# Left sides stored one pair later, residual rows fetched one by one, low parts on VectorE: a decoder block on one core

## The chip, the cores and the metric

One core of a Trainium2 chip runs the kernel. The metric is device time in microseconds (us) of one execution; lower is better. Engines are named as in the profile: PE is TensorE (matmuls), DVE VectorE, ACT ScalarE, POOL GpSimd, SP the engine whose queue issues nearly all DMAs.

## The reference, cut to what matters

A decoder block: an SSD branch and a differential-attention branch are gated and merged, `w_out` adds them to the residual stream `h`, and a SwiGLU FFN and a last norm follow. The change touches the FFN alone, in float32, with 1024 tokens, `D_MODEL` = 1024 and `D_FF` = 2816:

```python
    h = h + merged @ w_out[l]
    u2 = rmsnorm(h, norm_ffn_g[l])
    h = h + (jax.nn.silu(u2 @ w_gate_ffn[l]) * (u2 @ w_up_ffn[l])) @ w_down_ffn[l]
out = rmsnorm(h, norm_final_g)
return out[:, PAD_FRONT + N_META:]
```

## The kernel before, in words

**Precision.** A float32 product is made of three fp32r matmuls: an operand is cast to a high part (hi, whi, dhi) on ACT, and the difference, the low part (lo, wlo, dlo), is made on POOL or DVE; hi by hi, lo by hi and hi by lo go into the same PSUM bank. `split_to(dst, src, eng)` (L919 the cast, L920 the low part on engine `eng`) does this.

**Gate and up.** The 2816 hidden columns are 11 pairs of 128 columns. For each pair `Weights` loads the 1024 x 256 block of `w_gate_ffn` or `w_up_ffn` in two halves (L948), `raw` tiles of 512 KB. The halves make a 2 x 2 block matrix (A11, A12, A21, A22), the tokens, normed and transposed, another, and the block product is made with seven products in place of eight, as Strassen's method does. `Weights.make` builds the seven left operands: 1, 2, 5, 6 and 7 are sums or differences of two blocks (L986, on DVE, into a `sm` tile), 3 and 4 are blocks themselves; each goes through `split_to`, with POOL for the low part. `Half.product` (L1000) runs the 12 matmuls (128 x 512) of one product, and `Half.run` adds the products' banks into the quarter tiles (L1015 on ACT, L1017 to L1026 on DVE). Product 3 goes into the bank of product 5, so it waits until L1017 has read that bank; likewise product 7 waits for L1022, and product 4 for L1015. `gate_out` takes silu on ACT (L1039 to L1042), `up_out` multiplies (L1045 to L1048). A pair is 168 matmuls.

**Left sides of down.** The down product too is made with seven products, from blocks of the hidden matrix G (pairs by token halves). `left_sides` makes five sums of its quarters on DVE (L1058, L1061, L1063 to L1065) and stores seven row blocks in the DRAM tile `hid_d`: three of 256 KB (L1059, L1062, L1066) and one of 1 MB (L1067).

**Down.** 77 steps: products 1, 5, 4, 7, 3, 2, 6, each over the 11 pairs. A step loads a row block of `hid_d` (`ra`, L1250) and one or two quarters of `w_down_ffn` (`rb`, L1259 and L1262), sums the quarters (L1270), splits both and runs 12 matmuls. Steps 0 to 2 are loaded and made in the last pair, and steps 3 and 4 are loaded there; the others use the pool `dn`, opened after step 2's matmuls. Its tiles are the eight residual rows `hr` (512 KB each, from `h_d`, L1347), the final gain `gf` (L1350), five `ra` and `rb` buffers, four of `dhi` and `dlo`. When a product's 11 steps are done, its banks are added into the rows (L1363), one addition a step of the next product. In the loop `dn_load(s + 4)` loads four steps ahead.

**What sets the order.** Tiles are allocated from rings of a few buffers: `raw` of the first weight half has two, of the second one (ring `ht`, four of whose five hold a token side), G and U two, `tmp` three, and a write waits for the last reader of the old content. A scheduler orders the instructions of each engine at build time. On the chip each engine runs its list in that order, and so does SP with the DMAs.

Of the kernel before, what the change touches and what calls it, by code (L numbers as in the profile page):

```python
# [9 lines left out]
F32 = mybir.dt.float32  # L10
F32R = mybir.dt.float32r
AF = mybir.ActivationFunctionType
ALU = mybir.AluOpType
# [4 lines left out]
P = 128  # L18
D = 1024
# [4 lines left out]
NT = SEQ // P  # L24
# [18 lines left out]
def tile_hybrid_block(  # L43
# [7 lines left out]
    nc = tc.nc  # L51
# [9 lines left out]
    def nm(s):  # L61
        seq[0] += 1
        return f"{s}_{seq[0]}"
# [69 lines left out]
    h_d = dram([SEQ, D], "h_d")  # L133
    hid_d = dram([7, FF // 2, 512], "hid_d")
# [113 lines left out]
    def gates_block(b):  # L248
# [9 lines left out]
        out=gbh, in0=par[:, PR_GB : PR_GB + 16], scalar1=0.5, scalar2=None, op0=ALU.mult  # L258
# [3 lines left out]
        out=g08, in0=par[:, PR_SUB : PR_SUB + 1], scalar1=1.0 - LAM_INIT, scalar2=None,  # L262
# [4 lines left out]
    with tc.tile_pool(name="ssd", bufs=1, reuse_waits="tile") as sp:  # L267
# [4 lines left out]
        def t2(name, tag="t2", bufs=4):  # L272
# [6 lines left out]
            out=tri, in_=tri, pattern=[[1, P]], compare_op=ALU.is_ge, fill=0.0, base=0,  # L279
# [637 lines left out]
    def split_to(dst, src, eng):  # L917
        hi, lo = dst
        nc.scalar.copy(hi, src)  # L919
        eng.tensor_tensor(out=lo, in0=src, in1=hi.bitcast(F32), op=ALU.subtract)  # L920
# [15 lines left out]
    class Weights:  # L936


        def __init__(self, w, pair):
            self.w, self.pair, self.m, self.two_ = w, pair, {}, {}  # L940
            self.load()
# [30 lines left out]
        def make(self, *which):  # L972
            for i in which:
                self.m[i] = dst = self.slot(i)
                if i in (3, 4):
                    split_to(dst, (self.A11, self.A22)[i - 3], nc.gpsimd)
                    continue
                a, b, op = {
                    2: (self.A21, self.A22, ALU.add),
                    5: (self.A11, self.A12, ALU.add),  # L980
                    1: (self.A11, self.A22, ALU.add),
                    6: (self.A21, self.A11, ALU.subtract),
                    7: (self.A22, self.A12, ALU.subtract),
                }[i]
                tmp = tmp512("sm").rearrange("p (k c) -> p k c", c=P)
                vtt(out=tmp, in0=a, in1=b, op=op)  # L986
                split_to(dst, tmp, nc.gpsimd)

    class Half:

# [41 lines left out]
    def gate_banks():  # L1032
        return ps_mm(), ps_mm(), ps_sc(), ps_sc()
# [18 lines left out]

    SLOT = {1: 0, 2: 1, 5: 2, 6: 3, 3: 4, 4: 5, 7: 6}

    def left_sides(G, U, pair):
        rows = slice(pair * P, (pair + 1) * P)
        a11, a12, a21, a22 = G[:, 0, T1], G[:, 1, T1], G[:, 0, T2], G[:, 1, T2]
        vtt(out=U[:, 0, T2], in0=a21, in1=a22, op=ALU.add)  # L1058
        nc.sync.dma_start(hid_d[SLOT[4], rows, :], a22)  # L1059
        d = fp.tile([P, 512], F32, tag="tmp", name=nm("d"), bufs=3)  # L1060
        vtt(out=d, in0=a12, in1=a22, op=ALU.subtract)  # L1061
        nc.sync.dma_start(hid_d[SLOT[7], rows, :], d)  # L1062
        vtt(out=U[:, 0, T1], in0=a11, in1=a22, op=ALU.add)  # L1063
        vtt(out=U[:, 1, T1], in0=a11, in1=a12, op=ALU.add)
        vtt(out=U[:, 1, T2], in0=a21, in1=a11, op=ALU.subtract)  # L1065
        nc.sync.dma_start(hid_d[SLOT[3], rows, :], a11)  # L1066
        nc.sync.dma_start(  # L1067
            hid_d[0:4, rows, :].rearrange("s p t -> p s t"),
            U.rearrange("p a (b t) -> p (a b) t", t=512),
        )  # L1070

    def w_out_rows(t, before_last=None):
        hts = []
# [81 lines left out]
    G, U = new_pair()  # L1155
# [83 lines left out]
    up_w.make(7)  # L1239
    up.run(7)  # L1240
    up_out(G, U, up, 0)
    left_sides(G, U, 0)

    NP = NF // 2
    downs = [(i, f) for i in (1, 5, 4, 7, 3, 2, 6) for f in range(NP)]
# [51 lines left out]
    for pair in range(1, NP):  # L1297
        G, U = new_pair()
        last = pair == NP - 1
        for w in (w_gate_ffn, w_up_ffn):  # L1300
            gate_side = w is w_gate_ffn
            A = Weights(w[0], pair)
            A.make(*order7)
            h = Half(A, G if gate_side else U, (gate_banks if gate_side else up_banks)())
            if last and not gate_side:
                for s, pool in ((0, st), (1, wk)):
                    down_load(s, f512(fp, "tmp", 3), f1k(st, "raw", 2))
                    down_make(s, f512(fp, "tmp", 3), *pair_of(pool))
                h.run(*order7[:5])
                down_load(2, f512(fp, "tmp", 3), f1k(st, "raw", 2))  # L1310
                down_make(2, f512(fp, "tmp", 3), *pair_of(st))
                h.run(*order7[5:])
                for s in (3, 4):
                    down_load(s, f512(st, "gt", 2), f1k(st, "raw", 2))
            else:
                h.run(*order7)
            if gate_side:
                gate_out(G, h)
            else:
                up_out(G, U, h, pair)  # L1320
                left_sides(G, U, pair)

    b4 = gate_banks()
    for s in range(3):
        down_mm(downs, b4, [(s, j) for j in range(4)])
# [4 lines left out]
    with tc.tile_pool(name="dn", bufs=1, side="right", reuse_waits="tile") as dn:  # L1330
# [7 lines left out]
        def dn_load(s):  # L1338
            if s < len(downs) and s > 4:
                down_load(s, f512(dn, "ra", 5), f1k(dn, "rb", 5))  # L1340
# [2 lines left out]
        dn_make(4)  # L1343
        rows = []
        for r in range(NT):
            ht = dn.tile([P, D], F32, name=f"hr{r}")
            nc.sync.dma_start(ht, h_d[r * P : (r + 1) * P, :])  # L1347
            rows.append(ht)
        gf = dn.tile([P, D], F32, name="gf")
        nc.sync.dma_start(gf, norm_final_g.partition_broadcast(P))  # L1350
        for s in range(5, 9):
            dn_load(s)
        parts = {
            1: ((0, 0, 1), (1, 1, 1)), 2: ((1, 0, 1), (1, 1, -1)), 3: ((0, 1, 1), (1, 1, 1)),
            4: ((0, 0, 1), (1, 0, 1)), 5: ((0, 0, -1), (0, 1, 1)), 6: ((1, 1, 1),),
# [28 lines left out]
        def store(r, n):  # L1384
            nc.sync.dma_start(out2[r * P : (r + 1) * P, N2[n]], jks[r][:, N2[n]])
# [17 lines left out]
        for p in range(7):  # L1403
            i = downs[p * NP][0]
            banks = b4 if p == 0 else (up_banks if p % 2 else gate_banks)()
            for f in range(3 if p == 0 else 0, NP):
                s = p * NP + f
                dn_load(s + 4)
                if s + 2 < len(downs) and s + 2 > 4:
                    dn_make(s + 2)  # L1410
                if p < 6 or f < NP - 2:
                    down_mm(downs, banks, [(s, j) for j in range(4)])
                elif f == NP - 1:
                    down_mm(downs, banks, [(q, j) for j in range(4) for q in (s - 1, s)])
                for _ in range(2 if i in (2, 6) else 1):
                    if later:
                        later.pop(0)()
            for t, n, sign in parts[i]:
                for j in range(4):
                    if p < 6:  # L1420
                        later.append(
                            lambda a=(i, banks[j], j, t, n, sign): add_part(*a)
                        )
            if i == 3:
                later += [lambda r=r: first_rows(r) for r in range(4)]
            if i == 2:
                for j in range(4):
                    later.append(lambda r=4 + j: (square(r, 0), gain(r, 0, nc.gpsimd)))
# [62 lines left out]
```

## Time and profile before

| what | value |
|---|---|
| median of 3 runs | 2026.34 us (2026.12 to 2028.18) |
| the profiled execution, its own time | 2029.1 us |
| its span, first to last instruction | 2026.7 us |
| PE, DVE, ACT, POOL busy | 1923.2, 1252.8, 762.1, 567.1 us |
| mean granted clock of PE | 0.983 |
| DMA bytes | 241.38 MB |

The span runs from the first instruction to the last; the execution's own time has 2.4 us around it. A view by windows gives each engine's busy time in stretches of the span, with the clock that PE was granted (1.00 is 2.4 GHz, 0.50 is 1.2). A view by time lists an engine's instructions with the idle time before each, and what released it. A matmul's end is modelled: the distance from start to start is its pace.

### The profile page before, as it was taken

The numbers are of one execution on the slowest core, as the hardware profiler recorded it, in microseconds if no ns is written. First come the engines' busy times: TensorE is split into PE (matmuls) and PEld (weight loads), VectorE is DVE, ScalarE is ACT, GpSimd is POOL, SyncE is SP. The second block draws the span as 40 slices with busy tenths as digits, with TensorE's granted clock in tenths as the row PEclk, the third lists the DMA queues.
The fourth block names the chain that finished last, engine by engine and source line by source line (L and its number), as shares of the span: only waits on it lengthen the run. The fifth ranks groups of instructions, "written<-read, shape, count | busy, mean of one in ns | idle before, by whom it ended". The sixth has DMA issues, their size and how long they took to land.

```text
span 2026.7 us, 27727 instructions
## 1 busy us (share of the span) xinstructions
PE 1923.2 (95%) x10478; PEld 1668.0 (82%) x10478; DVE 1252.8 (62%) x2387; ACT 762.1 (38%) x1443; POOL 567.1 (28%) x363
## 2 busy tenths in 40 slices
PE   7999999999999999999999999889999998969998
PEld 7999777789999999888978899767777776758886
DVE  5656678555766566654663443585566656648887
ACT  5333222245555455553331124532222222224454
POOL 2223444411111111110122244344444544400002
PEclk9999999999999999999999999999999999989999
DMA  5111344311111211123765444322322232368865
GB/s 174 49 33 53 97 140 133 112 45 50 53 45 46 61 51 40 51 68 121 253 226 173 151 156 160 111 89 84 93 78 92 80 113 85 114 250 304 313 218 198
DMA packets 185935, 241.38 MB, mean 119 GB/s; under 512 B 13517, under 2 KB 128442, under 8 KB 185802
## 3 DMA queue, kind: packets, MB, share of 16 engines
q1 hardware_dynamic: 185658, 239.09, 36.7%
q8 instruction: 82, 1.34, 0.3%
q10 hardware_dynamic: 144, 0.52, 0.1%
q14 instruction: 51, 0.42, 0.1%
HBM read 181.48 MB, written 53.84 MB: 116 GB/s over the span
## 4 chain that ended last, share of the span: by engine, by line
PE 77%; DVE 13%; DMA 6%; issue 1%; ACT 1%; POOL 0%; SPq 0%; DVEq 0%; POOLq 0%; ACTq 0%
PE mm L108 14%; PE mm L109 14%; PE mm L110 14%; PE sc L1000 5%; PE tp L1000 4%; DVE sm L986 3%; DMA raw<-in_w_up_ffn_dram 3%; PE mm L1000 3%; PE sc L109 2%; PE sc L108 2%; PE sc L110 2%; PE tp L729 2%; PE sc L681 1%; PE sc L684 1%; PE sc L529 1%
## 5 line engine op out<-in xcount | busy, mean ns | idle before, releaser
L89 POOL TENSOR_TENSOR wlo<-raw,whi 128x1024 fp32r<-128x1024 f32 x68 | 176.4, 2594 | 685.8 <-ACT whi L87 614.3
L108 PE MATMUL mm<-uTh,whi 128*128 128x346 f32 (+2 forms) x1008 | 360.4, 358 | 7.5 <-DVE kl L626 2.4
L109 PE MATMUL mm<-uTh,wlo 128*128 128x346 f32 (+2 forms) x1008 | 359.5, 357 | 0.0
L110 PE MATMUL mm<-uTl,whi 128*128 128x346 f32 (+2 forms) x1008 | 358.8, 356 | 0.0
L108 PEld LDWEIGHTS mm<-uTh,whi 128*128 128x128 f32 x1008 | 190.9, 189 | 28.5 <-issue 8.4
L110 PEld LDWEIGHTS mm<-uTl,whi 128*128 128x128 f32 x1008 | 191.0, 189 | 18.7 <-issue 3.9
L109 PEld LDWEIGHTS mm<-uTh,wlo 128*128 128x128 f32 x1008 | 190.9, 189 | 17.7 <-issue 3.4
L920 POOL TENSOR_TENSOR wlo<-sm,whi 128x512 fp32r<-128x512 f32 x88 | 129.7, 1493 | 161.9 <-ACT whi L919 161.9
L919 ACT CAST whi<-sm 128x512 fp32r<-128x512 f32 x88 | 52.7, 619 | 215.4 <-DVE sm L986 95.8
L700 ACT ACTIVATE S<-S,mx 128x272 f32<-128x272 f32 (+7 forms) x128 | 101.0, 791 | 54.7 <-DVE mx L696 53.1
L986 DVE TENSOR_TENSOR sm<-raw,raw 128x512 f32<-128x512 f32 x66 | 54.6, 864 | 67.8 <-DMA raw<-in_w_up_ffn_dram 64.5
L920 POOL TENSOR_TENSOR lo<-raw,hi 128x512 fp32r<-128x512 f32 x44 | 65.5, 1488 | 88.8 <-ACT hi L919 88.8
L87 ACT CAST whi<-raw 128x1024 fp32r<-128x1024 f32 x68 | 71.2, 1047 | 50.6 <-PE mm L110 41.9
L748 DVE TENSOR_TENSOR atl<-tp,ath 128x512 fp32r<-128x512 f32 (+1 forms) x80 | 50.5, 634 | 61.8 <-ACT ath L747 61.5
L986 DVE TENSOR_TENSOR sm<-raw 128x512 f32<-128x512 f32 x44 | 50.6, 1154 | 58.7 <-DMA raw<-in_w_gate_ffn_dram 37.7
L1000 PE MATMUL mm<-t2a,hi 128*128 128x512 f32 x176 | 65.8, 433 | 21.8 <-DVE gu L1017 17.7
L919 ACT CAST dhi<-ra 128x512 fp32r<-128x512 f32 x72 | 44.7, 621 | 109.8 <-issue 53.6
L689 DVE CUSTOM_DVE_ANT_0 S<-sc,base 128x272 f32<-128x272 f32 (+7 forms) x128 | 62.0, 493 | 28.2 <-PE sc L684 27.0
L681 PE MATMUL sc<-k,q 128*128 128x144 f32 (+6 forms) x224 | 76.7, 349 | 1.7 <-ACT S L700 1.1
L689 DVE CUSTOM_DVE_ANT_0 S<-sc,base,mx 128x348 f32<-128x348 f32 (+4 forms) x96 | 56.1, 585 | 34.6 <-PE sc L684 31.2
L108 PE MATMUL mm<-whi,uTh 128*128 128x256 f32 x256 | 73.9, 290 | 3.5 <-ACT whi L100 3.3
L109 PE MATMUL mm<-whi,uTl 128*128 128x256 f32 x256 | 74.8, 293 | 0.1
(398 smaller groups left out, 5200.7 us busy)
## 6 DMA issues: line engine op xcount, KB each, us to landing
raw<-in_w_in_dram SPq DMA_DIRECT2D x60, 512.0 KB, 4.0
rb<-in_w_down_ffn_dram SPq DMA_DIRECT2D x82, 256.0 KB, 5.4
ra<-hid_d SPq DMA_DIRECT2D x74, 256.0 KB, 4.6
raw<-in_w_gate_ffn_dram SPq DMA_DIRECT2D x24, 512.0 KB
raw<-in_w_up_ffn_dram SPq DMA_DIRECT2D x24, 512.0 KB, 5.8
hid_d<-gu SPq DMA_DIRECT2D x11, 1024.0 KB, 5.1
rb<-in_w_down_ffn_dram SPq DMA_DIRECT2D x22, 512.0 KB, 6.3
bcs<-acs_d SPq DMA_DIRECT2D x16, 512.0 KB, 5.0
```

The lines of the kernel that those rows point to most:

```text
L87: nc.scalar.copy(hi, raw)
L89: nc.gpsimd.tensor_tensor(out=lo, in0=raw, in1=hi.bitcast(F32), op=ALU.subtract)
L108: nc.tensor.matmul(ps, lh, rh, start=first, stop=False)
L109: nc.tensor.matmul(ps, ll, rh, start=False, stop=False)
L110: nc.tensor.matmul(ps, lh, rl, start=False, stop=last)
L681: nc.tensor.matmul(ps[:, :w], qt[:, qs], kt[:, o : o + w], start=True, stop=False)
L689: nc.vector.tensor_tensor_reduce(out=S[:, o : o + w], in0=ps[:, :w], in1=base[:, L - W + o : L - W + o + w], scale=1.0, scalar=-3e38 if n ...
L700: nc.scalar.activation(S[:, :W], S[:, :W], AF.Exp, scale=slope, bias=nmx, accum_out=sm[:, comp : comp + 1],)
L919: nc.scalar.copy(hi, src)
L920: eng.tensor_tensor(out=lo, in0=src, in1=hi.bitcast(F32), op=ALU.subtract)
L986: vtt(out=tmp, in0=a, in1=b, op=op)
L1000: nc.tensor.matmul(ps, a[:, ki, :], b, start=first and ki == 0 and n == 0, stop=ki == KH - 1 and n == 2, skip_group_check=True,)
```

## The change

Three parts. `Weights.make` gives the low parts of the gate and up weights to DVE. `left_sides` becomes a class with two methods: the five sums of a pair are emitted behind the next pair's gate weights, and its four stores ahead of the next pair's up weights; after the last pair both follow at once. In the down stage the `hr` rows and `gf` are not fetched at the start: a row follows the loads at s = 5, 7 and 9, then one each step from s = 11, and `gf` comes at s = 33. And `dn_load(s + 4)` is left out for s = 3 and 4: those steps, 7 and 8, have been loaded just before.

```diff
@@ Weights.make
                 if i in (3, 4):
-                    split_to(dst, (self.A11, self.A22)[i - 3], nc.gpsimd)
+                    split_to(dst, (self.A11, self.A22)[i - 3], nc.vector)
                     continue
...
-                split_to(dst, tmp, nc.gpsimd)
+                split_to(dst, tmp, nc.vector)
@@ left_sides
-    def left_sides(G, U, pair):
-        rows = slice(pair * P, (pair + 1) * P)
...
+    class LeftSides:
+        def __init__(self, G, U, pair):
+            self.G, self.U, self.rows = G, U, slice(pair * P, (pair + 1) * P)
+
+        def sums(self):
+            G, U = self.G, self.U
+            a11, a12, a21, a22 = G[:, 0, T1], G[:, 1, T1], G[:, 0, T2], G[:, 1, T2]
+            self.d = fp.tile([P, 512], F32, tag="tmp", name=nm("d"), bufs=3)
+            vtt(out=U[:, 0, T2], in0=a21, in1=a22, op=ALU.add)
+            vtt(out=self.d, in0=a12, in1=a22, op=ALU.subtract)
+            vtt(out=U[:, 0, T1], in0=a11, in1=a22, op=ALU.add)
+            vtt(out=U[:, 1, T1], in0=a11, in1=a12, op=ALU.add)
+            vtt(out=U[:, 1, T2], in0=a21, in1=a11, op=ALU.subtract)
+
+        def store(self):
+            G, U, rows = self.G, self.U, self.rows
+            nc.sync.dma_start(hid_d[SLOT[7], rows, :], self.d)
+            nc.sync.dma_start(hid_d[SLOT[3], rows, :], G[:, 0, T1])
+            nc.sync.dma_start(hid_d[SLOT[4], rows, :], G[:, 1, T2])
+            nc.sync.dma_start(
+                hid_d[0:4, rows, :].rearrange("s p t -> p s t"),
+                U.rearrange("p a (b t) -> p (a b) t", t=512),
+            )
@@ the pair loop
-    left_sides(G, U, 0)
+    before = LeftSides(G, U, 0)
...
             A = Weights(w[0], pair)
+            if not gate_side:
+                before.store()
             A.make(*order7)
+            if gate_side:
+                before.sums()
...
-                left_sides(G, U, pair)
-
+                before = LeftSides(G, U, pair)
+
+    before.sums()
+    before.store()
@@ the down stage
         for r in range(NT):
-            ht = dn.tile([P, D], F32, name=f"hr{r}")
-            nc.sync.dma_start(ht, h_d[r * P : (r + 1) * P, :])
-            rows.append(ht)
+            rows.append(dn.tile([P, D], F32, name=f"hr{r}"))
         gf = dn.tile([P, D], F32, name="gf")
-        nc.sync.dma_start(gf, norm_final_g.partition_broadcast(P))
         for s in range(5, 9):
             dn_load(s)
+        fetch = [(rows[r], h_d[r * P : (r + 1) * P, :]) for r in range(NT)]
...
-                dn_load(s + 4)
+                if s > 4:
+                    dn_load(s + 4)
+                if s in (5, 7, 9) or s >= NP and fetch:
+                    nc.sync.dma_start(*fetch.pop(0))
+                if s == 3 * NP:
+                    nc.sync.dma_start(gf, norm_final_g.partition_broadcast(P))
```

The scheduler's new order shows best at three places. In the changed kernel the lines behind L1048 have moved: the five sums are L1065 to L1069, the stores L1073 to L1076, and in the down stage L1250, L1262 and L1347 have become L1259, L1271 and L1424.

DVE at a pair boundary, before, from the older pair's last product on (`gu` is G and U of a pair, the lower number the older pair):

```order
L1048 TENSOR_TENSOR gu_13911<-gu_13911 128x512
L986 TENSOR_TENSOR sm_14221<-raw_14197,raw_14199 128x512
L1063 TENSOR_TENSOR gu_13911<-gu_13911 128x512
L1064 TENSOR_TENSOR gu_13911<-gu_13911 128x512
L1065 TENSOR_TENSOR gu_13911<-gu_13911 128x512
L986 TENSOR_TENSOR sm_14340<-raw_14334,raw_14336 128x512
L986 TENSOR_TENSOR sm_14346<-raw_14334,raw_14336 128x512
L986 TENSOR_TENSOR sm_14358<-raw_14334,raw_14336 128x512
L986 TENSOR_TENSOR sm_14368<-raw_14336 128x512
L1017 TENSOR_TENSOR gu_14196<-mm_14236,gu_14196 128x512
```

and of the change, from the same product on:

```order
L1048 TENSOR_TENSOR gu_13901<-gu_13901 128x512
L920 TENSOR_TENSOR wlo_14363<-sm_14368,whi_14362 128x512
L920 TENSOR_TENSOR wlo_14339<-sm_14358,whi_14338 128x512
L1017 TENSOR_TENSOR gu_14186<-mm_14232,gu_14186 128x512
L1067 TENSOR_TENSOR gu_13901<-gu_13901 128x512
L1068 TENSOR_TENSOR gu_13901<-gu_13901 128x512
L1069 TENSOR_TENSOR gu_13901<-gu_13901 128x512
L920 TENSOR_TENSOR lo_2214_14208<-raw_14187,hi_2213_14207 128x512
L1019 TENSOR_TENSOR gu_14186<-mm_14231,gu_14186 128x512
L920 TENSOR_TENSOR lo_2231_14345<-sm_14346,hi_2230_14344 128x512
L986 TENSOR_TENSOR sm_14502<-raw_14472 128x512
```

L1017 of the new pair now stands ahead of the older pair's last three sums and of the next weight sum. The low parts (L920) stand among them. The last reader of `raw_14187` and the first of `raw_14472`, which takes its buffer, have two operations between them.

PE where product 3 joins product 5's bank (`mm_14236` before, `mm_14232` now), before:

```order
L1000 MATMUL sc_14238<-t2b,whi_14225 128x512
L1000 MATMUL sc_14372<-t1b,whi_14338 128x512
L1000 MATMUL mm_14236<-t2a,hi_2214_14217 128x512
L1000 MATMUL mm_14236<-t2a,lo_2215_14218 128x512
L1000 MATMUL mm_14236<-t2a,hi_2214_14217 128x512 x2
```

and of the change:

```order
L1000 MATMUL sc_14234<-t2b,whi_14215 128x512 x2
L1000 MATMUL mm_14232<-t2a,hi_2213_14207 128x512
L1000 MATMUL sc_14234<-t2b,wlo_14216 128x512
L1000 MATMUL sc_14234<-t2b,whi_14215 128x512 x2
...
L1000 MATMUL mm_14232<-t2a,lo_2214_14208 128x512
L1000 MATMUL mm_14232<-t2a,hi_2213_14207 128x512 x2
```

Product 6 (`sc_14234`) is cut in two around the first matmul of product 3, and the other eleven follow ten matmuls later.

SP at the start of the down stage, before:

```order
L1066 DMA hid_d<-gu_15336 128x512
L1067 DMA hid_d<-gu_15336 128x4x512
L1347 DMA hr_15733<-h_d 128x1024
...
L1347 DMA hr_15747<-h_d 128x1024
L1350 DMA gf<-in_norm_final_g_dram 128x1024
L1250 DMA ra_15751<-hid_d 128x512
L1262 DMA rb_15752<-in_w_down_ffn_dram 128x512 x2
```

and of the change:

```order
L1074 DMA hid_d<-gu_15326 128x512
L1076 DMA hid_d<-gu_15326 128x4x512
L1259 DMA ra_15742<-hid_d 128x512
L1271 DMA rb_15743<-in_w_down_ffn_dram 128x512 x2
...
L1259 DMA ra_15802<-hid_d 128x512
L1271 DMA rb_15803<-in_w_down_ffn_dram 128x512 x2
L1424 DMA hr_15733<-h_d 128x1024
```

The loads of steps 5 to 9 now follow the last store at once, and the first row comes behind them.

## Rows read from the trace of the kernel before

**Rows 1.** The page's first part: span, and busy time of each engine.

```profile
span 2026.7 us, 27727 instructions
PE 1923.2 (95%) x10478; PEld 1668.0 (82%) x10478; DVE 1252.8 (62%) x2387; ACT 762.1 (38%) x1443; POOL 567.1 (28%) x363
```

**Rows 2.** Windows; pair 1, first and eighth of eight pairs, last pair, down.

```profile
core 0: us, PE busy (x) PEld busy (x) DVE busy (x) ACT busy (x) POOL busy (x), PEclk, DMA share, GB/s
1343.13:1391.53 48.40, 41.45 (x169) 32.81 (x169) 30.50 (x36) 11.74 (x21) 21.31 (x15) 0.93 0.28 89
1391.53:1435.15 43.62, 40.14 (x168) 31.34 (x168) 26.88 (x32) 11.61 (x21) 21.15 (x14) 1.00 0.29 90
...
1701.95:1745.58 43.63, 40.19 (x168) 31.35 (x168) 26.59 (x32) 11.61 (x21) 21.13 (x14) 1.00 0.29 91
1745.58:1795.66 50.08, 48.08 (x204) 38.11 (x204) 34.15 (x41) 14.38 (x25) 18.25 (x12) 1.00 0.42 135
1795.66:1838.80 43.14, 26.02 (x103) 20.73 (x103) 19.46 (x31) 11.52 (x20) 0.00 (x0) 0.80 1.00 370
1838.80:1986.00 147.20, 147.20 (x651) 121.90 (x651) 120.40 (x195) 67.77 (x126) 4.16 (x4) 1.00 0.80 276
```

**Rows 3.** PE by time in one pair: start, duration, instruction, idle before it.

```profile
1466.41 0.40 PE L1000 MATMUL sc<-t1b,hi 128*128 128x512 f32 x1
1469.20 0.39 PE L1000 MATMUL tp<-t2a,hi 128*128 128x512 f32 x1
1475.00 0.50 PE L1000 MATMUL tp<-b,whi 128*128 128x512 f32 x1 [0.78 <-DVE gu L1022]
1478.76 0.50 PE L1000 MATMUL av<-t2b,whi 128*128 128x512 f32 x1 [0.71 <-ACT whi L919]
1498.42 0.53 PE L1000 MATMUL mm<-t2a,hi 128*128 128x512 f32 x1 [1.96 <-DVE gu L1017]
```

**Rows 4.** DVE by time in the same pair.

```profile
1463.86 0.69 DVE L986 TENSOR_TENSOR sm<-raw 128x512 f32<-128x512 f32 x1 [3.84 <-DMA raw<-in_w_gate_ffn_dram]
1480.55 1.78 DVE L986 TENSOR_TENSOR sm<-raw,raw 128x512 f32<-128x512 f32 x1
1482.25 1.78 DVE L1063 TENSOR_TENSOR gu<-gu 128x512 f32<-128x512 f32 x1
1494.18 1.90 DVE L986 TENSOR_TENSOR sm<-raw,raw 128x512 f32<-128x512 f32 x3 [6.75 <-DMA raw<-in_w_up_ffn_dram]
```

**Rows 5.** POOL by time in the same pair.

```profile
1458.62 1.30 POOL L920 TENSOR_TENSOR lo<-raw,hi 128x512 fp32r<-128x512 f32 x1 [0.40 <-ACT hi L919]
1481.74 1.74 POOL L920 TENSOR_TENSOR lo<-sm,hi 128x512 fp32r<-128x512 f32 x1
```

**Rows 6.** SP by time in the same pair: DMA issues.

```profile
1459.94 0.37 SPq L948 DMA_DIRECT2D raw<-in_w_gate_ffn_dram  x1
1477.76 0.34 SPq L1062 DMA_DIRECT2D hid_d<-d  x1
1487.46 0.37 SPq L1067 DMA_DIRECT2D hid_d<-gu  x1
1487.93 0.46 SPq L948 DMA_DIRECT2D raw<-in_w_up_ffn_dram  x1
```

**Rows 7.** PE by time at the start of the down stage.

```profile
1797.41 0.73 PE L108 MATMUL mm<-dhi 128*128 128x512 f32 x2 [1.75 <-ACT dhi L919]
1818.36 0.80 PE L108 MATMUL mm<-dhi 128*128 128x512 f32 x1 [15.19 <-ACT dhi L919]
```

**Rows 8.** SP by time at the start of the down stage.

```profile
1796.13 0.37 SPq L1067 DMA_DIRECT2D hid_d<-gu  x1
1796.61 5.39 SPq L1347 DMA_DIRECT2D hr<-h_d  x8
1805.46 0.32 SPq L1250 DMA_DIRECT2D ra<-hid_d  x1
```

**Rows 9.** DVE by time at the start of the down stage, with POOL silent.

```profile
1798.43 1.29 DVE L920 TENSOR_TENSOR dlo<-bs,dhi 128x512 fp32r<-128x512 f32 x2
1816.57 0.69 DVE L1270 TENSOR_TENSOR bs<-rb 128x512 f32<-128x512 f32 x1
```

**Rows 10.** The page's sixth part, DMA issues.

```profile
ra<-hid_d SPq DMA_DIRECT2D x74, 256.0 KB, 4.6
```

More of the change, by code (lines that the diff above doesn't have):

```diff
@@ L1053, in tile_hybrid_block @@
     SLOT = {1: 0, 2: 1, 5: 2, 6: 3, 3: 4, 4: 5, 7: 6}
-    def left_sides(G, U, pair):
-        rows = slice(pair * P, (pair + 1) * P)
[L1057 to L1070, printed above, removed]
+    class LeftSides:
[19 more added lines that the diff above has]
+            )
     def w_out_rows(t, before_last=None):
```

## The prediction

> **What bounds the kernel now.** I read the page's first part, then a table by stage, then the lines of time of PE, DVE, POOL and SP in one stretch each. TensorE (PE) is busy for 95% of the span [rows 1], so time can only come from the stretches where it is not. The table shows two in the FFN [rows 2]. The first is the loop over the column pairs: eight pairs in a row, from 1391.53 to 1745.58, take 354.05 us, 44.26 each, for 168 matmuls of PE a pair. At the pace of an undisturbed stretch these need less: twelve matmuls on `t1b,hi` take 1469.20 - 1466.41 = 2.79 us [rows 3], 0.2325 each, and 651 matmuls of the down stage take 147.20 us [rows 2], 0.226 each; 168 of them are 38.0 to 39.1 us, and I take **38.8**. So each pair loses about 5.5 us. The second is the start of the down stage: 43.14 us with PE busy for 26.02 of them, at a mean granted clock of 0.80, where the long stretch behind it stands at 1.00 [rows 2].
>
> In a pair PE stands three times [rows 3]: 0.78 us for the sum of L1022, 0.71 us for a whi from ACT and 1.96 us for the sum of L1017. All three come late by way of DVE: an element-wise operation there takes 0.69 us, but 1.78 us while POOL makes a low part, which itself then takes 1.74 us against 1.30 [rows 4, 5]; and the sums that feed ACT and PE stand behind the left sides of the pair before and behind a sum that waits 6.75 us for weights [rows 4]. Of the missing 5.5 us the three holes are 3.45; the rest is the slow restart after each, and in some pairs a stretch at the lower clock.
>
> At the start of the down stage PE stands 1.75 us for step 3 and 15.19 us for step 5 [rows 7]. SP says why: behind the last left-side store (1796.13) it issues the eight residual rows, and the first load for step 5 leaves at 1805.46 [rows 8]; its weights are summed at 1816.57 and PE starts at 1818.36 [rows 7, 9].
>
> **The change part by part.**
>
> *Low parts on DVE.* Per pair POOL loses its 14 operations and DVE gains 14. DVE then has 45 a pair: 10 weight sums, 14 low parts, 16 sums and products out of PSUM, 5 left sides. With POOL silent none should take 1.78 us; a row to row distance of 0.605 us is what operations of 0.69 us have when nothing holds them (two of them span 1.29) [rows 9]. That is 45 x 0.605 = **27.2 us** of 38.8, no more than DVE is busy now (26.9, [rows 2]). The price is the waits. Weight buffers are few, so each of a pair's four loads is issued only when DVE has made the last low part from the old content, and DVE's fixed order then reaches a sum of the new content two to five operations later and waits there with everything behind it. A load alone takes 3.90 us: issued at 1459.94, as POOL let go at 1459.92, used at 1463.86 [rows 4, 5, 6]. One issued behind a store of 1 MB takes 6.25 us: 1487.93 to 1494.18 [rows 4, 6]. With n operations between the releasing one and the reader the wait is 0.69 + landing - 0.605 x (n + 1). In the new order n is 2 for the gate side's first half (behind the 1 MB store): 5.1 us; 2 for its second half: 2.8; 5 and 3 for the up side's: 1.0 and 2.2. The difference d has a store of its own before its buffer is reused, with n = 3: the store issued at 1477.76 held nothing up at 1480.55 [rows 4, 6], so at most 2.8 us, a wait of 1.0. Sum 12.1 us, and 27.2 + 12.1 = **39.3 us**: DVE with its loads is then a loop as long as PE's own 38.8. I take 39.5 a pair, since PE's waits and DVE's will not overlap perfectly; the bounds are 38.8 (PE alone) and 44.3 (nothing gained).
>
> *Left sides one pair later.* The five sums are neither more nor fewer. They leave the place ahead of the next pair's L1017, where now three of 1.78 us stand; in the new order L1017 comes ahead of three of them, and PE has 28 matmuls of other products between product 5 and product 3, 6.4 us in which L1017 can be made; L1022 has some 4 to spare. The stores move on SP too, behind the up side's weights and ahead of the next gate weights; the 1 MB one now slows that gate load, which is the 5.1 us above. The G and U buffers, two deep, are held half a pair longer; their last store is out some 12 us into the next pair, 26 us before the buffer is written again: nothing.
>
> So eight pairs: 8 x (44.26 - 39.5) = **38 us**. Pair 1 (48.40 us, [rows 2]) has the same three causes and a filling pipeline: to 40.5, **8 us**. Pair 0 stays as it is, since DVE makes the token sides there and is full without a gap; only the first gate weights of pair 1 come sooner: **2 us**. The last pair with steps 0 to 2 (204 matmuls, 47.1 us at the same pace, against 50.08): **3 us**.
>
> *Residual rows one by one.* Ahead of step 5 go 8 rows and the final gain, 9 x 0.52 = 4.7 MB. Also, the loads of steps 7 and 8 were issued twice (74 loads into `ra`, where steps 5 to 76 need 72, [rows 10]): 2 x 0.79 = 1.6 MB less. In the new order step 5's loads follow the last store at once. The stretch moved 370 GB/s at a DMA share of 1.00 [rows 2], so 1.05 MB of store and 0.79 MB of loads are there in 5 us, and 1.8 us after landing (1816.57 to 1818.36, [rows 7, 9]) PE can go; it has steps 3 and 4, 5.4 us, to do meanwhile, and the store itself comes earlier by some 2 us because the last product of the pair is now issued 12 matmuls sooner. Both holes go. What is late next: the rows go between the loads of steps 9 to 15, and by 370 GB/s what must land up to step 15 (13.1 MB) takes 35.4 us, plus 1.8, where PE asks for step 15 after 34.5 (the 2 us, and twelve steps of 2.71): a stall of 2.7 us, wherever it falls. So 43.14 becomes 8 x 2.71 + 2.7 = 24.4: **19 us**. Bounds: 21.5 (no stall) and 5 (step 5 still late, or rows in the way).
>
> By the Trainium skill, page "DMA: Bandwidth & Descriptors", section Bandwidth, transfers between HBM and SBUF are bound at about 358 GB/s on the HBM side. By it the stall would be an estimated 3.9 us instead of 2.7, and the sum 1 us worse; the row shows 370, so the measurement decides, and the page is right that little room is left.
>
> **Sum.** 38 + 8 + 2 + 3 + 19 = 70 us, off the profiled execution's own 2029.1 us: 1959. The median of the runs is 2.8 us lower; I give **1958**.
>
> **The rivals.**
>
> *The loads bind the pairs (16%).* If each of the three free loads lands 1.7 us later, as it would when it meets one of the small stores, the loop is 39.3 + 5.1 = 44.4, and the eight pairs and pair 1 gain nothing. For it: the four loads of a pair wait one after another on one engine, and the store is now close to them. Against: DMA share in the pairs is 0.29 [rows 2]. Time: 2026.3 - 2 - 3 - 19 = 2002; half of it, 1980.
>
> *The down stage stays late (11%).* SP issues in order and waits for buffers; if the first loads wait for a pool that PE frees late, or a row's add holds DVE, 5 of 19 us come. Time: 1958 + 14 = 1972.
>
> *DVE turns into the bound (4%), slower.* One mechanism, in the pair loop: all loads land like the one behind the store or worse. The other parts give 24 us, 2.4 over each of ten pairs, so it decides from a loop of 46.7 us, each of the four loads 1.8 us later than taken. At 3.9 us later for each, 54.9 us: 8 x (54.9 - 44.3) = 85 lost, 24 kept: 2087.
>
> *It doesn't do what it says (3%):* the waits only change their names, 2026, as before.
>
> **How the numbers follow.** The forecast's own case (pairs at 38.8 to 41, down start cured) has 66%: 1945 to 1973. With the late down stage, and the better half of the binding loads, that makes 85%: **1944 to 1992**. A measurement of this kernel tells 0.2%, 4 us, from no change. Faster by more: 0.93; same: 0.03; slower: 0.04.
>
> **What would show it.** Right: POOL empty in the pairs; no DVE operation of 1.7 us there; PE's gaps before L1017's and L1022's readers gone; pairs 39 to 40 us apart, clock 1.00; DVE waiting 10 to 12 us a pair for loads; the first matmul of step 5 without a hole. Wrong: a pair over 42 us with DVE waiting for weights while PE waits for DVE (the loads bind), or a hole over 5 us before step 5 or between steps 9 and 16 (the rows still in the way).

## The result, and the profile after

The changed kernel takes 1954.17 us, median of 4 runs (1952.70 to 1955.78), against 2026.42 us of the kernel before in the same comparison: a ratio of 0.964, 95% interval 0.9625 to 0.9659. The forecast was 1958, in a range of 1944 to 1992.

The page's first part, which answers to [rows 1]:

```profile
span 1954.1 us, 27632 instructions
PE 1900.7 (97%) x10478; PEld 1664.0 (85%) x10478; DVE 1261.9 (65%) x2541; ACT 766.0 (39%) x1443; POOL 335.2 (17%) x209
```

DVE has 154 instructions more and POOL 154 fewer (11 pairs of 14), and yet DVE is busy only 9 us longer. To see where 72.6 us of span went I cut both traces by matmuls: back from the first matmul of step 3, 36 of steps 0 to 2, then 168 for each pair. The windows of the kernel before at these cuts, pair 0 and pairs 2 to 9 (columns as in [rows 2], which have pair 1, pair 10 with steps 0 to 2, and the start of down at the same cuts):

```profile
1291.20:1343.13 51.93, 42.41 (x170) 30.91 (x168) 43.12 (x61) 28.58 (x47) 17.37 (x12) 0.90 0.16 47
1391.53:1745.58 354.05, 326.09 (x1344) 254.12 (x1344) 214.00 (x249) 92.89 (x161) 169.68 (x112) 0.99 0.29 89
```

and of the changed kernel, pair 0, pair 1, pairs 2 to 9, pair 10 with steps 0 to 2, and the start of down:

```profile
1287.63:1341.97 54.34, 43.81 (x169) 31.89 (x168) 47.77 (x78) 29.26 (x49) 0.00 (x0) 0.87 0.18 52
1341.97:1380.66 38.69, 38.69 (x170) 31.60 (x168) 30.22 (x50) 11.93 (x20) 0.00 (x0) 1.00 0.33 104
1380.66:1689.63 308.97, 308.97 (x1345) 252.76 (x1344) 222.97 (x360) 95.98 (x160) 0.00 (x0) 1.00 0.33 103
1689.63:1736.40 46.77, 46.77 (x205) 38.35 (x204) 32.67 (x53) 13.87 (x24) 0.00 (x0) 1.00 0.46 147
1736.40:1765.65 29.25, 26.08 (x103) 21.00 (x102) 19.30 (x31) 11.11 (x19) 0.00 (x0) 0.88 1.04 383
```

| stretch | before | after | gain | forecast |
|---|---|---|---|---|
| ahead of pair 0 | 1291.2 | 1287.6 | 3.6 | 0 |
| pair 0 | 51.9 | 54.3 | -2.4 | 2 |
| pair 1 | 48.4 | 38.7 | 9.7 | 8 |
| pairs 2 to 9 | 354.1 | 309.0 | 45.1 | 38 |
| pair 10, steps 0 to 2 | 50.1 | 46.8 | 3.3 | 3 |
| start of down, 102 matmuls | 43.1 | 29.3 | 13.9 | 19 |
| the rest | 187.9 | 188.5 | -0.6 | 0 |

From pair 1 to step 2 PE is busy in every microsecond, at the full clock: 38.6 us a pair. The first line of the table is no work of the change: the code ahead of the FFN is the same, and in the traces of this study pair 0 began anywhere from 1286.3 to 1291.2. The kernel before happened to be traced at the late end.

In a pair, DVE by time (compare [rows 4]; L1017, the sum that PE stood for, is the third row):

```profile
1410.47 0.69 DVE L986 TENSOR_TENSOR sm<-raw 128x512 f32<-128x512 f32 x1 [1.45 <-DMA raw<-in_w_up_ffn_dram]
...
1419.53 0.69 DVE L986 TENSOR_TENSOR sm<-raw 128x512 f32<-128x512 f32 x1 [1.29 <-DMA raw<-in_w_up_ffn_dram]
...
1427.11 0.68 DVE L1017 TENSOR_TENSOR gu<-mm,gu 128x512 f32<-128x512 f32 x1
...
1436.21 0.69 DVE L986 TENSOR_TENSOR sm<-raw 128x512 f32<-128x512 f32 x1 [4.81 <-DMA raw<-in_w_gate_ffn_dram]
1436.82 0.68 DVE L1020 TENSOR_TENSOR gu<-mm,gu 128x512 f32<-128x512 f32 x1
...
1441.95 1.90 DVE L986 TENSOR_TENSOR sm<-raw,raw 128x512 f32<-128x512 f32 x3 [2.52 <-DMA raw<-in_w_gate_ffn_dram]
```

The four waits for loads, 1.45, 1.29, 4.81 and 2.52, are those forecast as 1.0, 2.2, 5.1 and 2.8; the store of d holds nothing up. PE's first matmul of product 3 (the second row here) starts 4.2 us after L1017 starts, without a gap (compare the last row of [rows 3]):

```profile
1430.88 0.62 PE L1000 MATMUL sc<-t2b,whi 128*128 128x512 f32 x2
1431.34 0.40 PE L1000 MATMUL mm<-t2a,hi 128*128 128x512 f32 x1
```

The one gap left from pair 1 to the last matmul of the down stage is at step 5 of the down stage (compare [rows 7]): 3.17 us.

```profile
1745.18 0.79 PE L108 MATMUL mm<-dhi 128*128 128x512 f32 x1 [3.17 <-ACT dhi L919]
```

Behind it the granted clock falls to 0.50 (1.2 GHz) for 5.7 us, in which 14 matmuls start, by a window:

```profile
1745.18:1750.89 5.71, 5.71 (x14) 4.45 (x14) 5.33 (x10) 2.96 (x6) 0.00 (x0) 0.50 1.05 390
```

SP by time there (compare [rows 8]): the 1 MB store waits for the last left-side sum (DVE, 1733.83 to 1734.52), and step 5's loads stand behind it.

```profile
1734.54 0.37 SPq L1076 DMA_DIRECT2D hid_d<-gu  x1
1735.02 0.44 SPq L1259 DMA_DIRECT2D ra<-hid_d  x1
```

ACT by time: step 5's left side at 1740.45, then a wait for step 6's left side, and only behind that step 5's right side, whose sum (DVE, 1742.04) had been there for 1.8 us.

```profile
1740.45 0.62 ACT L919 CAST dhi<-ra 128x512 fp32r<-128x512 f32 x1 [4.07 <-DMA ra<-hid_d]
1743.99 0.62 ACT L919 CAST dhi<-ra 128x512 fp32r<-128x512 f32 x1 [2.92 <-DMA ra<-hid_d]
1744.51 0.61 ACT L919 CAST dhi<-bs 128x512 fp32r<-128x512 f32 x1
```

### The profile page after: what moved, and what is told of

It is laid out like the page before. It is cut to its first block, busy times and chain, and to the rows that moved or that the text cites. A ratio compares the mean times of both kernels' runs of the same rounds, so it can differ in the third digit from the quotient of the medians.

```text
span 1954.1 us, 27632 instructions
## 1 busy us (share of the span) xinstructions
PE 1900.7 (97%) x10478; PEld 1664.0 (85%) x10478; DVE 1261.9 (65%) x2541; ACT 766.0 (39%) x1443; POOL 335.2 (17%) x209
## 4 chain that ended last, share of the span: by engine, by line
PE 90%; DVE 5%; DMA 2%; ACT 1%; issue 1%; POOL 0%; SPq 0%; POOLq 0%; DVEq 0%; ACTq 0%
PE mm L108 15%; PE mm L109 15%; PE mm L110 15%; PE sc L1000 8%; PE mm L1000 6%; PE tp L1000 6%; PE sc L109 2%; PE sc L108 2%; PE sc L110 2%; PE tp L729 2%; PE av L1000 2%; PE sc L529 1%; PE sc L681 1%; PE sc L684 1%; PE av L109 1%; PE av L110 1%
## 5 line engine op out<-in xcount | busy, mean ns | idle before, releaser
L1393 POOL TENSOR_TENSOR ss<-ss,mhalf 128x1 f32<-128x1 f32 x8 | 6.9, 874 | 605.5 <-DVE ss L1389 605.3
L689 DVE CUSTOM_DVE_ANT_0 S<-sc,base 128x272 f32<-128x272 f32 (+7 forms) x128 | 62.0, 493 | 27.9 <-PE sc L684 26.7
L110 PE MATMUL mm<-wlo,uTh 128*128 128x256 f32 x256 | 73.5, 288 | 0.7 <-DVE wlo L102 0.7
L684 PE MATMUL sc<-kl,q 128*128 128x144 f32 (+6 forms) x224 | 72.1, 325 | 0.0
L424 DVE SCALAR_TENSOR_TENSOR hh<-raw,cwh,hh 128x1040 f32<-128x1040 f32 x36 | 69.4, 1927 | 1.1
L1000 PE MATMUL mm<-t2a,hi 128*128 128x512 f32 x176 | 61.7, 402 | 5.6 <-ACT t2a L1141 2.2
```

What stands on the lines that cost most here:

```text
L110: nc.tensor.matmul(ps, lh, rl, start=False, stop=last)
L424: nc.vector.scalar_tensor_tensor(out=hh[:, :L], in0=raw[:, k : k + L], scalar=cwh[:, b, k : k + 1], in1=hh[:, :L], op0=ALU.mult, op1=ALU.add,)
L684: nc.tensor.matmul(ps[:, :w], qt[:, qs], kl[comp][:, o : o + w], start=False, stop=True,)
L689: nc.vector.tensor_tensor_reduce(out=S[:, o : o + w], in0=ps[:, :w], in1=base[:, L - W + o : L - W + o + w], scale=1.0, scalar=-3e38 if n ...
L1000: nc.tensor.matmul(ps, a[:, ki, :], b, start=first and ki == 0 and n == 0, stop=ki == KH - 1 and n == 2, skip_group_check=True,)
```

## The experiments

**One part at a time.** Four kernels take one part of the change each; the edits are those of the change's own diff. All four stood against the same runs of the kernel before (2027.64 us).

*Low parts on DVE alone.*

```diff
-                    split_to(dst, (self.A11, self.A22)[i - 3], nc.gpsimd)
+                    split_to(dst, (self.A11, self.A22)[i - 3], nc.vector)
...
-                split_to(dst, tmp, nc.gpsimd)
+                split_to(dst, tmp, nc.vector)
```

> The kernel before with one part of the change: the low parts of the gate and up weights on DVE, the rest as it was. Theory (two delays that each part cures in half): no DVE operation of 1.7 us is left in the pairs, so PE's gaps for the whi cast (0.71 us) and for L1022 (0.78) go, but L1017 still stands behind three left sides, four weight sums and now low parts, fourteen operations of 0.6 us from the older pair's last product, so a gap of 1 to 3 us for it stays: pairs 40.5 to 42 us apart, 2026 - 10 x 2.5 = about 2000 (1992 to 2008). Rival (the contention is all): pairs 38.5 to 39, 1970 to 1976. Rival (the order is all): pairs stay over 43, 2020 or more. The hole before step 5 of the down stage stays at 15 us in each.

2001.1 us, ratio 0.9866 (0.9851 to 0.988). Total as the first theory had it, but by other gaps. Pairs 2 to 9 take 338.3 us, 42.3 each, in turn some 40 and 44. The gap for L1017 is gone. That of 0.71 us for a whi cast, which was to go, stays in four of the eight pairs, and in the other four PE by time has these two:

```profile
1634.36 0.51 PE L1000 MATMUL tp<-b,whi 128*128 128x512 f32 x1 [1.98 <-DVE gu L1022]
1638.39 0.50 PE L1000 MATMUL mm<-t1b,whi 128*128 128x512 f32 x1 [1.00 <-ACT whi L919]
```

DVE by time: a weight sum waits for its load, but that wait does not make the gap, for behind it DVE stands 0.93 us more, for PE.

```profile
1630.80 0.69 DVE L986 TENSOR_TENSOR sm<-raw 128x512 f32<-128x512 f32 x1 [2.62 <-DMA raw<-in_w_up_ffn_dram]
1632.42 0.69 DVE L1020 TENSOR_TENSOR gu<-tp,gu 128x512 f32<-128x512 f32 x1 [0.93 <-PE tp L1000]
1633.03 0.68 DVE L1046 TENSOR_TENSOR gu<-gu,tp 128x512 f32<-128x512 f32 x1
1633.62 0.68 DVE L1022 TENSOR_TENSOR gu<-tp,gu 128x512 f32<-128x512 f32 x1
```

By the times, PE ended L1022's product with the first of these matmuls and L1020's with the second:

```profile
1629.19 0.40 PE L1000 MATMUL tp<-t2b,whi 128*128 128x512 f32 x1
1631.99 0.40 PE L1000 MATMUL tp<-t2a,hi 128*128 128x512 f32 x1
```

So L1022 is late by its place in DVE's list, behind L1020, whose product PE made last.

*Left sides one pair later alone* (the diff's class, its calls, and nothing else).

> The kernel before with one part of the change: the left sides summed and stored one pair later, low parts still on POOL, rows fetched as before. Theory (two delays): L1017 comes ahead of three left sides, so its gap of 1.96 us goes; DVE operations beside a POOL low part still take 1.78 us, so the gaps of 0.7 to 0.8 us for the whi cast and for L1022 stay or move: pairs 41.5 to 43 us apart, 2026 - 10 x 1.9 = about 2007 (2000 to 2016). Rival (the order is all): pairs 38.5 to 39, 1970 to 1976. Rival (the contention is all): pairs stay over 43, 2020 or more.

1980.79 us, ratio 0.9771 (0.9755 to 0.9787): much more than expected. Pairs 2 to 9 take 320.3 us, 40.0 each, 39.2 the best. The gaps for L1022 and for the whi cast, which I had put down to the contention, are gone too. The trace of the kernel before shows that the contention did not make them, in the pair of [rows 3]:

```profile
1474.25 0.69 DVE L1022 TENSOR_TENSOR gu<-tp,gu 128x512 f32<-128x512 f32 x1 [0.77 <-PE tp L1000]
...
1477.04 0.69 DVE L1061 TENSOR_TENSOR d<-gu 128x512 f32<-128x512 f32 x1
1477.64 1.28 DVE L986 TENSOR_TENSOR sm<-raw,raw 128x512 f32<-128x512 f32 x2
...
1478.79 2.99 POOL L920 TENSOR_TENSOR wlo<-sm,whi 128x512 fp32r<-128x512 f32 x2 [8.93 <-ACT whi L919]
```

POOL is idle until 1478.79, and DVE's operations take 0.69 us. L1022 runs as soon as PE has made its product, and PE's next product, 7, is the one that waits for L1022; the weight sums for the whi cast stand behind a pair's first two left sides (L1058, L1061). In the changed kernel 26 matmuls of other products stand between that product's last matmul and product 7's first:

```profile
1413.67 0.39 PE L1000 MATMUL tp<-t2b,whi 128*128 128x512 f32 x1
1419.82 0.40 PE L1000 MATMUL tp<-b,whi 128*128 128x512 f32 x1
```

So what cures this gap is the new order of PE's products, which the scheduler chose. No run keeps the order and changes the operations' times alone. What is left of the contention in the run with the left sides alone, DVE by time, with POOL busy throughout:

```profile
1590.19 0.68 DVE L1017 TENSOR_TENSOR gu<-mm,gu 128x512 f32<-128x512 f32 x1
1590.79 1.19 DVE L1067 TENSOR_TENSOR gu<-gu 128x512 f32<-128x512 f32 x1
1591.91 1.78 DVE L1068 TENSOR_TENSOR gu<-gu 128x512 f32<-128x512 f32 x1
```

and its effect, a gap like this one in two of the eight pairs, where PE waits for POOL itself:

```profile
1596.56 0.50 PE L1000 MATMUL mm<-t2a,lo 128*128 128x512 f32 x1 [1.24 <-POOL lo L920]
```

*Rows one by one and single loads, alone.*

> The kernel before with the two parts of the change in the down stage alone: rows fetched one by one, and the loads of steps 7 and 8 issued once. Theory (the parts add): the hole of 15.19 us before step 5 shrinks as it did in the whole change, whose trace has 3.17 us there; the 103 matmuls that took 43.1 us take some 29 to 31, pairs stay at 43.7 by count of matmuls: 2026 - 13 = 2013 (2010 to 2016). Rival (it pays only because the pairs before it are faster and the last store comes sooner): at most 5 us, 2021 or more.

2014.29 us, ratio 0.9934 (0.9919 to 0.995): as the first theory, in full without the faster pairs. The gap before step 5 falls from 15.19 to this:

```profile
1804.44 0.50 PE L108 MATMUL mm<-dhi 128*128 128x512 f32 x1 [3.56 <-ACT dhi L919]
```

*Single loads alone.*

```diff
-                dn_load(s + 4)
+                if s > 4:
+                    dn_load(s + 4)
```

> The kernel before without the second issue of the loads of steps 7 and 8 (72 loads into ra in place of 74), all else as it was. Theory (the eight rows ahead of step 5 make the hole): step 5 still starts behind 15 us, since the doubled loads come after its own; at most the 1.6 MB less, 4 us at 390 GB/s, helps where step 7 or 9 would wait: 2023 to 2027, no change that can be told or little. Rival (the doubled loads make half of the late start): 2018 or less.

2026.88 us, ratio 0.9994 (0.9984 to 1.0003): no change. The gap is as it was; with the run before this one, the rows made it:

```profile
1816.83 0.80 PE L108 MATMUL mm<-dhi 128*128 128x512 f32 x1 [15.11 <-ACT dhi L919]
```

Together: pairs 1 to 10 take 444.2 us before, 421.7 with the low parts alone (22.6 less), 402.8 with the left sides alone (41.4 less), 386.3 with both (58.0 less). Added, the two give 64.0, 6.0 more than both together; both also cure the gap of 1.75 us before step 3, which counts once. By the medians the low parts give 26.5 us, the left sides 46.9, the rows 13.4: 86.7 together, 14.5 more than the whole. The 6.0 of the pairs and 1.9 of steps 0 to 2 are counted twice in that; the rest I can't assign, and it is of the size by which the start of the FFN differs from trace to trace. The run with the left sides alone moves the five sums and the four stores together, so their shares stay open.

**Does DVE's loop bind?** A second 1 MB store a pair, ahead of the gate load:

```diff
+    again_d = [dram([4, FF // 2, 512], f"again_d{q}") for q in range(1)]
...
+            if rows.stop < FF // 2:
+                for q_d in again_d:
+                    nc.sync.dma_start(
+                        q_d[0:4, rows, :].rearrange("s p t -> p s t"),
+                        U.rearrange("p a (b t) -> p (a b) t", t=512),
+                    )
```

> The changed kernel with each pair's 1 MB of left sides stored a second time, into a DRAM tile that nobody reads; in eight of the pairs both stores stand right ahead of the next pair's first gate load, and DVE's list there is as in the changed kernel. The load, 6.2 us behind one store, should land 2.4 us later, and DVE's wait for it go from 4.8 to 7.2 us. Theory of the prediction (DVE with its loads is a loop nearly as long as PE's own: 27.2 us of work, 10.1 us of waits for loads, 1.4 of waits for PE, of 38.6): 1 to 1.5 us of the 2.4 show, pairs 39.3 to 40.5 us apart, gaps of PE for DVE or ACT return: 1962 to 1974. Rival (PE alone sets the pace and the waits are spare time): pairs stay at 38.6, 1953 to 1957.

1955.3 us, ratio 0.9642 (0.9626 to 0.9658): as the rival. Eight pairs, by a window:

```profile
1381.38:1690.29 308.91, 308.91 (x1345) 252.74 (x1344) 224.21 (x361) 96.10 (x160) 0.00 (x0) 1.00 0.41 132
```

The same 38.6 us, with a DMA share of 0.41 in place of 0.33. DVE by time (this kernel's lines are one higher here, L1021 is the changed kernel's L1020):

```profile
1553.09 0.69 DVE L1021 TENSOR_TENSOR gu<-mm,gu 128x512 f32<-128x512 f32 x1 [5.79 <-PE mm L1001]
1553.79 0.69 DVE L921 TENSOR_TENSOR lo<-raw,hi 128x512 fp32r<-128x512 f32 x1
1554.40 0.69 DVE L1023 TENSOR_TENSOR gu<-sc,gu 128x512 f32<-128x512 f32 x1
1555.00 0.68 DVE L987 TENSOR_TENSOR sm<-raw 128x512 f32<-128x512 f32 x1
```

In these pairs DVE's list was not quite the changed kernel's: the scheduler put the sum of the new weights three places back. So a later load in the same list was not tried. But the rows show what the 4.81 us of the changed kernel are: without them DVE waits 5.79 us at the same place, for PE's product 3. The wait for the load lies beside a wait for PE that is there anyway.

**The gap before step 5.** The changed kernel itself ran again beside the next two.

> The changed kernel once more, to stand beside the next two on the same chip: 1951 to 1957, with a hole of 3.2 us before step 5 of the down stage and 17 us from step 3's first matmul to step 7's.

1956.22 us (1954.2 to 1957.79); gap 3.15 us; 17.06 us from the first matmul of step 3 to that of step 7, of which some 11 are matmuls at full pace.

*Right side split first:*

```diff
-        split_to((hi[:, 0], lo[:, 0]), ra, nc.vector)
         split_to((hi[:, 1], lo[:, 1]), b, nc.vector)
+        split_to((hi[:, 0], lo[:, 0]), ra, nc.vector)
```

> The changed kernel, but in each down step the right side (the weights) is split ahead of the left side (the rows of hid_d), in the order of the program. In the changed kernel ACT's list has the cast of step 6's ra ahead of that of step 5's bs, and waits 2.92 us for the load of step 6 while the sum for step 5 is done; here step 5's two casts stand ahead of step 6's. Theory (ACT's order makes half of the hole): bs is cast at 1742.8 in place of 1744.5, so the hole before step 5 goes from 3.2 to 1.5 us, perhaps another for step 6: 1.5 to 4 us less in the stretch of steps 3 to 6, total 1 to 4 us less than changed_again. Rival (the loads alone make it: step 6's come no sooner): the wait goes from step 5 to step 6, and the stretch stays within 1 us.

1953.41 us (1950.59 to 1956.73). PE by time:

```profile
1741.15 0.50 PE L108 MATMUL mm<-dhi 128*128 128x512 f32 x1 [1.45 <-ACT dhi L919]
1744.51 0.73 PE L110 MATMUL mm<-dlo,dhi 128*128 128x512 f32 x2 [1.48 <-DVE dlo L920]
```

Steps 3 to 6 take 14.40 us. The 1.45 is as the theory had it; a second gap of 1.48 comes within step 5, for DVE has the sum of step 6's weights, whose load is late, ahead of step 5's low part:

```profile
1743.16 0.69 DVE L1279 TENSOR_TENSOR bs<-rb 128x512 f32<-128x512 f32 x1 [2.71 <-DMA rb<-in_w_down_ffn_dram]
1743.77 0.69 DVE L920 TENSOR_TENSOR dlo<-bs,dhi 128x512 fp32r<-128x512 f32 x1
```

Both views were half right. Of the 2.7 us that the stretch gains, 2.4 are PE's busy time, at a higher clock: with two gaps of 1.5 us the granted clock stays at 1.00 in this stretch, with one of 3.15 its mean is 0.80. The ranges of the two kernels' times overlap, so the gain is told by the traces alone.

```profile
1736.61:1753.67 17.06, 13.91 (x49) 10.90 (x48) 11.50 (x18) 5.82 (x10) 0.00 (x0) 0.80 1.03 368
```

```profile
1734.11:1748.51 14.40, 11.47 (x50) 8.86 (x49) 8.08 (x14) 5.01 (x10) 0.00 (x0) 1.00 1.03 366
```

(the first row is the changed kernel's second run, the other this kernel's).

*The last pair's stores on ACT's queue:*

```diff
-        def store(self):
+        def store(self, eng=nc.sync):
...
-            nc.sync.dma_start(hid_d[SLOT[7], rows, :], self.d)
+            eng.dma_start(hid_d[SLOT[7], rows, :], self.d)
...
-    before.store()
+    before.store(nc.scalar)
```

> The changed kernel, with the last pair's four stores issued from ACT's queue in place of SP's, so that SP's loads for step 5 no longer stand behind stores that wait for the last left-side sums (until 1734.5). Theory (SP's order makes the hole): step 5's three loads leave when their buffers are free, some us sooner, and land ahead of the 1 MB store: no hole before step 5, steps 3 to 6 in 11 to 13 us in place of 17, total 4 to 6 us less than changed_again; then the rows bind, a stall of at most 3 us between steps 9 and 16. Rival (the buffers bind: they come free only as the weights' last matmuls end): the loads leave within 1 us of 1735 again, the hole stays at 2 to 3.5 us, no change.

1952.02 us (1950.63 to 1955.77). SP by time: step 5's loads leave 16.7 us ahead of step 3's first matmul (1739.03), in place of 1.4, so no buffer held them there, only the stores ahead of them on SP.

```profile
1722.31 0.37 SPq L1259 DMA_DIRECT2D ra<-hid_d  x1
1722.72 2.38 SPq L1271 DMA_DIRECT2D rb<-in_w_down_ffn_dram  x2
```

The gap is gone: steps 3 to 6 take 11.02 us. What is late next is what the forecast had as its stall at step 15, PE by time:

```profile
1772.66 0.50 PE L108 MATMUL sc<-dhi 128*128 128x512 f32 x1 [0.69 <-ACT dhi L919]
```

Steps 3 to 76 take 202.2 us in place of 207.2; the median is 4.2 less than that of the changed kernel beside it, with ranges that overlap a little. On ACT's queue the stores hold ACT's casts, which costs little here: the first cast of step 3 stands behind the last store, and step 3 starts with a gap of 0.13 us.

**A faster version.** With the stores on ACT's queue, the low parts of pair 0 alone on POOL again, and in the second kernel the right side first as well:

```diff
+            low = nc.vector if self.pair else nc.gpsimd
...
-                split_to(dst, tmp, nc.vector)
+                split_to(dst, tmp, low)
```

> The changed kernel once more, beside the next two on the same chip: 1952 to 1958.

> The changed kernel with the last pair's stores on ACT's queue, as before, and with the low parts of pair 0 alone back on POOL. Theory (in pair 0 DVE is full with the token sides, and a POOL low part costs DVE less there than one of its own; the run with the left sides alone had pair 0 in 52.7 us, the changed kernel in 54.3): pair 0 in 52.5 to 53, pairs 1 to 10 at 38.5, the down stage as with the stores on ACT's queue: 6 to 7 us less than changed_third. Rival (in pair 0 the contention costs as much as it saves): 5 us less, from the stores alone.

> The same, and the right side split ahead of the left one in the down steps. Theory (with the loads in time ACT's order costs nothing): within 1 us of act_stores_pool_pair0. Rival (the casts' order still costs at steps 5 and 6): 1 to 2 us less than it.

Beside them the changed kernel takes 1954.1 us (1952.43 to 1954.42), the second kernel 1950.83 (1949.41 to 1952.33), and all three edits 1949.4 (1948.46 to 1952.13), ratio to the kernel before 0.9619 (0.9606 to 0.9632) against the changed kernel's 0.964 (0.9627 to 0.9653). That is less than the 6 to 7 us expected. Pair 0 takes 51.8 and 51.2 us, against 53.2 to 54.4 in the traces of the changed kernel, but pair 1 takes 40.0 in place of 38.7: the two make 91.8 and 91.2, against 91.9 in the trace beside them and 93.0 in the other two, so POOL there is worth at most 2 us, and whether it is worth anything stays open. The order of the casts makes no difference that shows.

## Why the prediction was right

**What bounded the pairs: right.** 44.3 us were PE's own 38.8 and its waits; without the waits 38.6 are left. The list of what would show it holds for the pairs: POOL is empty there, the gaps for L1017 and L1022 are gone, and the clock is at 1.00. For step 5, which was to start without a hole, it does not.

**The weight of the two causes: only partly right.** I told the gaps for L1022 and for the whi cast to the contention. Run by itself the later left sides remove both and are worth 41.4 us in ten pairs, the low parts 22.6, and in the kernel before POOL is idle where both gaps arise. As far as the rows show, they come from the order of the lists of PE and DVE, which is another in each of these kernels; the prediction's first reading, three waits by way of DVE, holds in part, as L1022 itself was not late. For L1017 it holds, and there the contention has a part: three left sides of 1.78 us stand ahead of the 1 MB store, and behind that store the load that L1017's wait of 6.75 us goes back to ([rows 4, 6]). The contention itself is as read: the rows with POOL busy show 1.78 us for a sum of two SBUF tiles, and 0.68 for one of PSUM and SBUF. The Trainium skill, page "SBUF — State Buffer", section "Who interferes with whom", has it so: an operation of VectorE with two SBUF inputs contends with a GpSimd operation that reads SBUF, one with at most one SBUF input, outside the modes that use both of VectorE's port pairs, does not.

**"DVE with its loads is a loop as long as PE's own": the step that was off.** Its numbers came near (10.1 us of waits against 12.1, 27.9 us of work against 27.2), the conclusion did not: I added waits and work as if DVE had nothing else to wait for. The run with two stores shows that it waits for PE in the same time. So 39.5 us a pair was 0.9 us too long, 7.1 us over pairs 2 to 9. A second megabyte in front of the gate load costs nothing, in the list that the scheduler made for it; with the changed kernel's own list that was not run.

**Pair 0, pair 1, the last pair:** -2.4, 9.7 and 3.3 us against 2, 8 and 3. Pair 0 grew. The prediction had DVE full without a gap there, and yet put the low parts that DVE gains at nothing; with the low parts alone pair 0 takes 54.3 us too, with the left sides alone 51.4.

**The start of down: right in kind, 5 us too much.** Both holes were to go, with a stall of 2.7 at step 15. The hole before step 3 went (either change to the pairs removes it, the rows do not); that before step 5 stayed at 3.17 us, with the lower clock behind it 6.2 in all (29.25 less 102 matmuls of 0.226), and the stall did not come, as the loads won those 6 us. The step that failed is "PE has steps 3 and 4 to do meanwhile": store and loads took 7.5 us to land, not 5 (issued from 1734.54 on, the last of them summed at 1742.04), which by the 1.8 us from sum to matmul makes a hole of about 2; and ACT's order, which the prediction didn't weigh, had step 6's left side ahead of step 5's right side, so that step 5 waited for step 6's load as well. Once the loads go early, the stall at step 15 is there, about 1 us of the 2.7. One more part of the miss is a sum: the forecast counted eight steps, 96 matmuls, where the stretch of [rows 2] holds 102, so its 24.4 us should have been 25.8, and the gain 17. The stretch moved 383 GB/s, where [rows 2] show 370. The Trainium skill's bound of some 358 (page "DMA: Bandwidth & Descriptors", section Bandwidth) is exceeded in both kernels, so the measurement decided rightly.

The forecast of 1958 owes its closeness to two errors of opposite sign, and that is luck: 4.7 us too little in pairs 0 to 10 (51 forecast, 55.7 measured) and 5.1 too much at the start of down; the sum of the terms was 70, and 69.6 came from the same stretches.

## What to carry to other kernels

A wait for a load on an engine that also serves TensorE is to be set against the wait for TensorE at the same place, not added to its work: only what outlasts that wait costs. On an engine that works through a fixed list, look first at what stands ahead of the operation that frees a bank, and on PE at how soon the next product wants that bank. Here storing the left sides later, with the order that came of it, was worth nearly twice what the low parts on DVE were. A gap is to be laid to a stretched operation only where the trace shows one stretched just before it. On a queue, a store that waits for the last result holds every load behind it, though their buffers may have been free for 15 us; the store can go to another queue, where it holds what stands behind it there.

## What the runs showed of the hardware

Two gaps of PE of 1.5 us with matmuls between them left the granted clock at 1.00 (2.4 GHz) over the stretch; one of 3.15 to 3.17 us was followed by 5.7 to 5.8 us at 0.50 (1.2 GHz) in two traces of the changed kernel. There the wait cost twice what it lasted, where the two short ones, 2.9 us, cost 3.4. It is no rule of the gap's length alone: behind a gap of 3.18 us in the third trace of the changed kernel, and one of 2.96 us in the run with two stores, the clock was at 0.50 for 3.4 us only, and the kernel before has such a stretch behind three of its eight gaps for L1017 of 1.87 to 2.32 us (the third trace, then one of those):

```profile
1743.92:1747.33 3.41, 3.41 (x10) 2.55 (x9) 3.24 (x6) 2.16 (x4) 0.00 (x0) 0.50 1.06 395
1498.74:1502.15 3.41, 3.41 (x9) 2.63 (x8) 1.95 (x2) 0.79 (x2) 3.09 (x3) 0.50 0.03 5
```

And the DMA engines moved 383 GB/s over 29 us at the start of the down stage, with loads, a store and rows mixed, more than the 370 of the same place before.
